# A gather turned round, padded code between experts, and a ring of 21 weight tiles in a mixture-of-experts kernel

## The chip, the cores and the metric

The kernel runs on one core of one Trainium2 chip. The metric is device time in microseconds (us): 1147.12 us is the median of 3 runs of the kernel before (1146.0 to 1147.28). One execution was taken with the hardware profiler.

## The reference

One layer of a streaming encoder on 256 tokens of 1024 values, all in float32. A first half mixes tokens (a convolution and two kinds of attention behind one projection). The second half, on which nearly all of the time goes, is a mixture of 32 experts of which each token takes four:

```python
h2 = rms_norm(x, norm2_g) * (1 + scale2) + shift2
logits = (xt @ router_w + router_b).astype(jnp.float32)
top_vals, top_idx = lax.top_k(logits, TOP_K)          # TOP_K = 4 of 32
top_w = jax.nn.softmax(top_vals, axis=-1)
...
def expert_step(acc, params):
    w1, b1, w2, b2, gate_e = params
    u = xt @ w1 + b1                                  # w1: 1024 x 2048
    glu = jnp.minimum(u[:, ::2], SWIGLU_LIMIT)
    lin = jnp.clip(u[:, 1::2], -SWIGLU_LIMIT, SWIGLU_LIMIT)
    a = glu * jax.nn.sigmoid(SWIGLU_ALPHA * glu) * (lin + 1)
    out = a @ w2 + b2                                 # w2: 1024 x 1024
    return acc + gate_e[:, None] * out.astype(jnp.float32), None
...
return x + gate2 * moe_ffn(h2, ...)
```

## The kernel before

The first half runs from the start to about 183 us. It loads 24 tiles of `w_ada`, 12 of `w_in` and 4 of `w_out`, each 128 x 2048 float32 (1 MB), computes the modulation vectors on VectorE, and the mixers.

The second half is a loop over 32 experts. An expert has 12 weight tiles of 1 MB: eight of `w1` (`we{e}_0` to `we{e}_7`) and four of `w2` (`we{e}_8` to `we{e}_11`), 384 tiles in all. All these tiles, and the big tiles of the first half, live in one pool, the ring. It has 20 tiles of four kinds: `l` (loads of the first half), `h`, `x` and `c` (its intermediate results). `KINDS` (line 33) says how many of each there are, and the string `RING` (line 34) in which order the weight tiles go through them, so weight tile n takes the place of tile n - 20. `prefetch` (line 849) issues the loads on the SyncE queue (SP), in order: 20 before the loop, then 4 at the start of an expert and 8 near its end. Each load waits until the tile that it overwrites has been read for the last time, and until the load eight before it has landed.

A token sits in a slot of its expert. The main path of an expert works on the first 64 slots. In it, `first` (line 876) makes `u` from four `w1` tiles at a time, on two halves (`u{e}_0`, `u{e}_1`); `turned` (898) transposes the activations `a` into `aT`; `second` (906) makes `o` from the four `w2` tiles; VectorE multiplies `o` by the gate (line 1088). Every second expert, `scatter` (937) adds the results of two experts to the residual (`y`).

Before its main path an expert has a conditional block, `if_more` (1020): when more than 64 tokens chose the expert, `more` (957) does slots 65 to 96 in narrow products (32 columns of weights each), with all twelve tiles of the expert; nested inside stand further blocks for over 96, over 160 and over 224 tokens. The code of these blocks stands in the instruction stream between one expert's main path and the next, and is jumped over where it isn't needed. A branch hint (`hint`, line 803) at the start of an expert's main path tells TensorE's sequencer of the jump at its end.

The change's gather is in `Prepare`. For two experts at a time, a one-hot matrix `oh` (tokens x 2 x 64 slots) picks the tokens' normalised rows `xn2`. `gather` (line 734) computes the picked rows with the model's dimension on the partitions: for each of 8 blocks of 128 values and each of 2 token tiles, a block of `xn2` is the stationary operand and `oh` the moving one, 16 products of 128 x 128 into `self.ps`. `modulated2` (740) then applies scale and shift, and the result `xg` feeds `u`. `prepare` (797) is called inside odd experts for the next two, between `first` and `second`; for experts 0 and 1 the calls stand in the first half.

A scheduler sets the final order on each engine: it lets products run ahead or behind where their inputs are later, so the program's order is close to the written one, and not the same.

## Time and profile before

| What | Value |
|---|---|
| median of 3 runs | 1147.12 us (1146.0 to 1147.28) |
| the profiled execution's own time | 1146.89 us |
| its span, first to last instruction | 1144.9 us |
| TensorE (PE) busy | 1069.5 us, 93% of the span |
| VectorE (DVE) / ScalarE (ACT) busy | 389.2 us / 178.6 us |
| moved by DMA | 449.54 MB, mean 393 GB/s |
| granted TensorE clock, mean | 0.985 |

The span is cut into 40 slices of 28.6 us; a digit is a busy share in tenths. Matmuls overlap in the records, so the start of the next row is a better end for a row than its own length. "x16" counts instructions: a float32 product is two matmul instructions, a transpose one, and each has a weight load (PEld) of its own. The idle time in square brackets stands ahead of the row, with what ended it. "PEq" is TensorE's sequencer, and its line 1021 is the branch of `if_more`.

### The profile page before, as it was taken

To read this page: it belongs to the slowest core of one execution; us is meant where nothing else is said; L and a number is where in the kernel's file an instruction comes from. 1 tells how busy PE (TensorE), PEld (TensorE's weight loads), DVE (VectorE), ACT (ScalarE), POOL (GpSimd) and SP (SyncE) were. 2 spreads that over 40 slices of the span, in tenths; PEclk is the share of its full clock that TensorE was granted. 3 is DMA by queue.
4 is the path that set the end of the run, shared out by engine and by line. 5 is a ranking of instruction groups with operands and counts; after the bars stand their busy time and mean duration, and the time that the engine had idled before them with its cause. 6 is when DMAs were issued, how large, how long until landed. Compare 5 with 4: busy or idle time off the path is not lost. (4 is left out here: it accounts for less than half of the span.)

```text
span 1144.9 us, 14101 instructions
## 1 busy us (share of the span) xinstructions
PE 1069.5 (93%) x5432; PEld 467.1 (41%) x5432; DVE 389.2 (34%) x879; ACT 178.6 (16%) x412; POOL 14.5 (1%) x52
## 2 busy tenths in 40 slices
PE   2999999999989999999999989999999999898987
PEld 2887844343333333433333433434343434242322
DVE  7799933222232223222222222232232322231222
ACT  3458622010101010101010100101010101010100
POOL 1000000000000000000000000000000000000000
PEclk7899999999999999999999989999999999999999
DMA  9888899999987999999999999999999999999992
GB/s 383 360 297 311 331 409 370 416 418 417 418 353 309 417 418 417 418 418 417 417 418 416 419 399 404 419 418 418 417 417 419 417 418 417 411 416 410 416 413 110
DMA packets 62913, 449.54 MB, mean 393 GB/s; under 512 B 6960, under 2 KB 7472, under 8 KB 8624
## 3 DMA queue, kind: packets, MB, share of 16 engines
q1 hardware_dynamic: 62336, 447.11, 95.6%
q8 instruction: 79, 1.29, 0.5%
q10 hardware_dynamic: 432, 0.59, 0.1%
q14 instruction: 66, 0.54, 0.1%
HBM read 446.63 MB, written 1.05 MB: 391 GB/s over the span
## 5 line engine op out<-in xcount | busy, mean ns | idle before, releaser
L83 PE MATMUL u<-we,xg 128*64 128x512 f32 (+1 forms) x2304 | 494.2, 577 | 12.7 <-DMA we<-in_w 11.3
L83 PEld LDWEIGHTS u<-we,xg 128*64 128x64 f32 (+1 forms) x2304 | 154.0, 134 | 299.9 <-issue 260.4
L83 PE MATMUL o<-we,aT 128*64 128x512 f32 x1024 | 236.5, 598 | 3.7 <-DMA we<-in_w 3.3
L891 DVE TENSOR_SCALAR sw<-u 128x256 f32<-128x256 f32 (+1 forms) x68 | 28.3, 417 | 441.6 <-PE u L83 429.5
L892 ACT ACTIVATE sw<-sw 128x256 f32<-128x256 f32 (+1 forms) x68 | 27.9, 411 | 666.8 <-DVE sw L891 666.8
L83 PEld LDWEIGHTS o<-we,aT 128*64 128x64 f32 x1024 | 69.6, 136 | 133.2 <-issue 121.8
L1088 DVE TENSOR_TENSOR o<-o,g 64x512 f32<-64x512 f32 x64 | 44.1, 689 | 162.2 <-PE o L83 161.7
L83 PE MATMUL y<-o,sc 128*128 128x512 f32 (+1 forms) x160 | 67.1, 592 | 2.1 <-DVE o L1010 1.3
L83 PEld LDWEIGHTS xg<-oh,xn 128*128 128x128 f32 x512 | 58.6, 192 | 12.6 <-issue 12.4
L83 PE MATMUL xg<-oh,xn 128*128 128x128 f32 x512 | 62.1, 279 | 0.1
L236 DVE SCALAR_TENSOR_TENSOR a<-a,silurow 128x1024 f32<-128x1024 f32 x48 | 57.2, 1216 | 0.0
L745 DVE TENSOR_SCALAR xg<-xg,mods 128x128 f32<-128x128 f32 x64 | 26.0, 410 | 62.7 <-ACT xg L748 61.5
L83 PE MATMUL u<-b,pick 128*128 128x512 f32 x64 | 31.0, 484 | 17.3 <-PEq L1021 16.7
L83 PEld LDWEIGHTS y<-o,sc 128*128 128x128 f32 (+1 forms) x160 | 26.5, 197 | 41.8 <-issue 33.4
L944 DVE TENSOR_TENSOR xr<-xr,y 128x1024 f32<-128x1024 f32 x30 | 36.6, 1221 | 11.8 <-PE y L83 10.4
L904 ACT COPY aT<-aT 128x256 f32<-128x256 f32 x64 | 23.8, 372 | 106.1 <-PE aT L86 106.0
L748 ACT ACTIVATE xg<-xg,mods 128x128 f32<-128x128 f32 x64 | 28.9, 457 | 56.4 <-PE xg L83 45.9
L83 PEld LDWEIGHTS u<-b,pick 128*128 128x128 f32 x64 | 12.1, 189 | 57.1 <-issue 55.9
L86 PEld LDWEIGHTS aT<-ident,a 128*128 128x128 f32 x128 | 14.2, 141 | 50.7 <-issue 33.9
L895 DVE TENSOR_TENSOR a<-a,sw 128x256 f32<-128x256 f32 x64 | 27.4, 428 | 6.8 <-ACT sw L892 0.3
L86 PE MATMUL aT<-ident,a 128*128 128x128 f32 x128 | 27.2, 294 | 2.0
L83 PE MATMUL op<-o,yT 128*128 128x512 f32 x64 | 29.0, 600 | 0.0
(299 smaller groups left out, 750.3 us busy)
## 6 DMA issues: line engine op xcount, KB each, us to landing
we<-in_w SPq DMA_DIRECT2D x383, 1024.0 KB, 19.9
a<-in_ada SPq DMA_DIRECT2D x24, 1024.0 KB, 7.0
w<-in_win SPq DMA_DIRECT2D x12, 1024.0 KB, 11.0
o<-in_wout SPq DMA_DIRECT2D x4, 1024.0 KB, 5.8
xr<-in_x SPq DMA_DIRECT2D x1, 1024.0 KB, 5.3
we<-in_w SPq DMA_DIRECT2D x2, 512.0 KB, 18.1
b1in<-in_be SPq DMA_DIRECT2D x1, 512.0 KB, 5.3
out<-xr SPq DMA_DIRECT2D x2, 256.0 KB, 2.0
```

What stands on the lines that cost most here:

```text
L83: last[:] = [nc.tensor.matmul(out, lhsT, rhs, start=start, stop=stop, skip_group_check=True).ins]
L86: last[:] = [nc.tensor.transpose(out, in_, ident).ins]
L236: nc.vector.scalar_tensor_tensor(w[:, i], w[:, i], 1.0, silu_row, op0=ALU.mult, op1=ALU.mult, accum_out=mods[:, m, k:k + 1])
L745: nc.vector.tensor_scalar(o, x, s2[:, k:k + 1], t2[:, k:k + 1], op0=ALU.mult, op1=ALU.add)
L748: nc.scalar.activation(o, x, AF.Identity, scale=s2[:, k:k + 1], bias=t2[:, k:k + 1])
L891: nc.vector.tensor_scalar(gl, u[:, 0:n], 7.0, None, op0=ALU.min)
L892: nc.scalar.activation(sg, gl, AF.Sigmoid, scale=1.702)
L895: nc.vector.tensor_mul(ln, ln, sg)
L904: nc.scalar.copy(aT.rearrange("p j s -> p (j s)"), ps[:, 0:n])
L944: nc.vector.tensor_add(xr[:, t, :], xr[:, t, :], y.rearrange("p h m -> p (h m)"))
L1088: nc.vector.tensor_mul(o[64 * (e % 2):64 * (e % 2) + 64, 512 * h:512 * h + 512], ps[r, :], g2[r, :])
```

## The change

Three parts. The ring gets an eighth tile of kind `l`, 21 in all, with a new order. The gather of experts 2 to 31 (`beside`) makes `oh` the stationary operand and 512 columns of `xn2` the moving one: 4 products into a second pair of PSUM banks (`xs`), two copies of 128 x 512 to SBUF on ScalarE, and 8 transposes into the place where `gather` wrote. The innermost conditional block of each expert gets a given number of further transposes of the identity (`FILL`), which run only for an expert with over 224 tokens; they lengthen the code that is jumped over, so that main paths begin at multiples of 256 TensorE instructions.

```diff
-KINDS = {"l": 7, "h": 8, "x": 2, "c": 3}
-RING = "lhhllccchlhhhxhhlllx"
+KINDS = {"l": 8, "h": 8, "x": 2, "c": 3}
+RING = "llhhllccchhhhxxhhllll"
...
+FILL = (99, 1, 93, 100, 107, 116, 107, 115, 107, 116, 107, 115, 107, 116, 107, 115, 107, 116, 107, 115, 107, 116, 107, 115, 107, 116, 107, 115, 107, 116, 107, 0)
...
+        def beside(self):
+
+            at = pa(f"xs{self.e}")
+            for t in range(NT):
+                onehot(self.oh[:, t], 0, CAP, [self.e, self.e + 1], pos[:, t])
+            for h in range(2):
+                for t in range(NT):
+                    mm(at[:, h, :], self.oh[:, t].rearrange("p e c -> p (e c)"), xn2[:, t, h * 512:h * 512 + 512], t == 0, t == NT - 1)
+            for h in range(2):
+                xs = t2k(f"xs{self.e}_{h}")
+                nc.scalar.copy(xs, at[:, h, :])
+                for k in range(4):
+                    turn(self.ps[h][:, k * P:(k + 1) * P], xs[:, k * P:(k + 1) * P])
...
     def prepare(e):
         p = Prepare(e)
-        for t in range(NT):
-            p.half(t)
+        p.beside()
         p.rest()
...
             if blocks[1:]:
                 if_more(n_e, e, a, aT, blocks[1:])
+            elif FILL[e]:
+                fill = pb(f"fill{e}")
+                for _ in range(FILL[e]):
+                    turn(fill[:, 0:P], ident)
```

On TensorE, in the main path of expert 1, the gather for experts 2 and 3 stood before as one run between the second `u` and the first `o` (a row "x16" counts products here):

```order
L83 MATMUL u1_1_3021<-we1_7_1671,xg0_1602 64x512 x4
L83 MATMUL xg2_3061<-oh2_3060,xn2_246 128x128 x16
L86 MATMUL og2_3096<-ident_80,og2_3089 128x128 x2
L1051 TENSOR_LOAD cnt_1525
L83 MATMUL o1_3103<-we1_8_2372,aT1_0_2407 64x512 x4
L86 MATMUL aT1_1_3108<-ident_80,a1_1_3040 128x128 x2
L83 MATMUL o1_3103<-we1_9_2374,aT1_0_2407 64x512 x4
```

Now, on the same engine at the same place:

```order
L86 MATMUL u1_1_3125<-we1_7_1671,xg0_1602 64x512 x4
L86 MATMUL xs2_3166<-xn2_246,oh2_3164 128x512 x4
L89 MATMUL og2_3201<-ident_80,og2_3194 128x128 x2
L1071 TENSOR_LOAD cnt_1525
L86 MATMUL o1_3208<-we1_8_1673,aT1_0_2509 64x512
L89 MATMUL xg2_3165<-ident_80,xs2_0_3173 128x128 x4
L89 MATMUL xg2_3165<-ident_80,xs2_1_3179 128x128 x4
L86 MATMUL o1_3208<-we1_8_1673,aT1_0_2509 64x512 x3
L89 MATMUL aT1_1_3213<-ident_80,a1_1_3144 128x128 x2
L86 MATMUL o1_3208<-we1_9_2474,aT1_0_2509 64x512 x4
```

The gather is split: its products stay where they were, and the transposes stand behind one product of `o`, with the other three of that tile after them. Elsewhere TensorE's order is the same, but for the fill inside the blocks that are jumped over.

On SP's queue, the end of the first prefetch and the first branch before (`cnt` is the tile with the tokens' counts, which SP reads for its own branches):

```order
L858 DMA we1_6_1669<-in_w1 128x2048
L858 DMA we1_7_1671<-in_w1 128x2048
L1051 TENSOR_LOAD cnt_1525
L1021 COMPARE_AND_BRANCH x4
L1021 UNCONDITIONAL_BRANCH x5
```

And now:

```order
L874 DMA we1_6_1669<-in_w1 128x2048
L874 DMA we1_7_1671<-in_w1 128x2048
L874 DMA we1_8_1673<-in_w2 128x2048
L1071 TENSOR_LOAD cnt_1525
L1037 COMPARE_AND_BRANCH x4
L1037 UNCONDITIONAL_BRANCH x5
```

The 21st load, tile 8 of expert 1, moved ahead of SP's first branch; from the branch of expert 2 on, as many loads stand before each of SP's branches as before.

## Rows read from the trace of the kernel before

**Rows 1.** The page's picture of the span in 40 slices: TensorE, the DMA engines, and what they moved.

```profile
PE   2999999999989999999999989999999999898987
...
DMA  9888899999987999999999999999999999999992
GB/s 383 360 297 311 331 409 370 416 418 417 418 353 309 417 418 417 418 418 417 417 418 416 419 399 404 419 418 418 417 417 419 417 418 417 411 416 410 416 413 110
```

**Rows 2.** Busy time in six stretches of the loop over experts. Columns: stretch, its length, then busy us and instructions of PE, PEld, DVE, ACT and POOL, the granted clock, the DMA engines' busy share, GB/s.

```profile
183.00:323.00 140.00, 138.35 (x621) 52.27 (x620) 34.24 (x80) 14.38 (x34) 2.54 (x6) 1.00 1.00 411
323.00:349.00 26.00, 21.78 (x259) 10.09 (x259) 10.93 (x29) 1.42 (x5) 0.00 (x0) 0.93 0.63 259
370.00:650.00 280.00, 273.03 (x1250) 102.79 (x1246) 72.62 (x161) 25.89 (x65) 2.66 (x10) 1.00 1.01 418
650.00:705.00 55.00, 47.86 (x354) 18.64 (x352) 15.39 (x33) 3.00 (x9) 0.00 (x0) 0.91 0.99 400
...
975.00:1121.00 146.00, 130.23 (x572) 45.87 (x570) 32.49 (x70) 11.63 (x30) 0.53 (x2) 1.00 1.01 411
1121.00:1134.00 13.00, 11.05 (x49) 3.25 (x47) 1.60 (x4) 0.79 (x2) 0.00 (x0) 1.00 0.07 30
```

**Rows 3.** TensorE in order of time: the first row of the extra block of expert 5 and, behind its last, the start of the expert's main path. Columns: start, length, operation, instructions, idle time ahead.

```profile
323.00 1.07 PE L83 MATMUL xg<-xn,ox 128*32 128x256 f32 x16
...
344.68 0.47 PE L83 MATMUL u<-b,pick 128*128 128x512 f32 x1 [0.67 <-PEq L1021]
345.08 8.75 PE L83 MATMUL u<-we,xg 128*64 128x512 f32 x32
```

**Rows 4.** What SP's queue waited for between 300 and 360 us: line, whom it waited for, us in total, times, the longest.

```profile
SPq L858 <- PE u L83: 45.2, 13, 24.2
```

**Rows 5.** The DMA view of 335 to 352 us, in 40 slices of 0.425 us.

```profile
GB/s 386 386 501 366 405 405 328 308 251 212 154 96 96 77 19 0 0 0 0 0 0 0 39 0 19 0 0 0 0 0 0 0 0 0 154 77 270 386 424 443
```

**Rows 6.** The chain of waits at the end of the span: start, length, what.

```profile
1112.57 19.88 DMA we<-in_w
1132.44 0.14 issue
1132.58 3.67 PE o L83 x16
...
1136.27 0.69 DVE o L1088
...
1137.01 3.91 PE y L83 x8
```

**Rows 7.** TensorE in order of time through a gather (expert 1, for experts 2 and 3).

```profile
226.61 3.84 PE L83 MATMUL xg<-oh,xn 128*128 128x128 f32 x32
230.28 0.38 PE L86 MATMUL og<-ident,og 128*128 128x128 f32 x2
230.60 1.94 PE L83 MATMUL o<-we,aT 128*64 128x512 f32 x8
232.47 0.44 PE L86 MATMUL aT<-ident,a 128*128 128x128 f32 x2
```

**Rows 8.** TensorE in order of time at two places with operations like the new ones: eight transposes in the first half, and four products with 512 moving columns in a scatter.

```profile
162.33 1.04 PE L86 MATMUL h2ps<-ident,xr 128*128 128x128 f32 x8
163.28 3.70 PE L83 MATMUL op<-o,yT 128*128 128x512 f32 x8
...
304.31 3.70 PE L83 MATMUL y<-o,sc 128*128 128x512 f32 x8
307.85 0.38 PE L86 MATMUL aT<-ident,a 128*128 128x128 f32 x2
```

**Rows 9.** Groups of ScalarE operations on 128 x 512, from PSUM and from SBUF: busy us, mean ns of one, idle time ahead.

```profile
L178 ACT ACTIVATE qksq<-qkss,epsc 128x512 f32<-128x512 f32 x6 | 4.1, 686 | 2.8 <-PE qkss L83 2.8
L324 ACT ACTIVATE qksq<-pr 128x512 f32<-128x512 f32 x6 | 3.6, 599 | 11.4 <-PE pr L83 11.4
```

**Rows 10.** TensorE's waits at the branch over the whole span, and the rows in order of time behind the branches of experts 1 to 4 and 10.

```profile
PE u L83 <- PEq L1021: 16.7, 30, 2.0
...
206.78 3.64 PE L83 MATMUL o<-we,aT 128*64 128x512 f32 x14 [0.28 <-PEq L1021]
238.60 0.47 PE L83 MATMUL u<-b,pick 128*128 128x512 f32 x1 [0.40 <-PEq L1021]
268.64 0.49 PE L83 MATMUL u<-b,pick 128*128 128x512 f32 x1 [0.30 <-PEq L1021]
296.90 0.47 PE L83 MATMUL u<-b,pick 128*128 128x512 f32 x1 [0.41 <-PEq L1021]
485.82 0.47 PE L83 MATMUL u<-b,pick 128*128 128x512 f32 x1 [1.99 <-PEq L1021]
```

**Rows 11.** Every wait for a DMA by TensorE, VectorE or ScalarE in the first half (0 to 183 us), by the waits of that stretch.

```profile
ACT silu L216 <- DMA p<-in_p: 3.1, 1, 3.1
ACT win0h L109 <- DMA w<-in_win: 3.0, 1, 3.0
ACT win6h L109 <- DMA w<-in_win: 3.0, 1, 3.0
DVE gains L293 <- DMA p<-in_p: 2.6, 1, 2.6
ACT xn L263 <- DMA xr<-in_x: 0.7, 1, 0.7
```

**Rows 12.** TensorE's waits for projection weights in the first half, the largest near 91 us.

```profile
90.62 0.39 PE L83 MATMUL pr<-hTh,win5h 128*128 128x256 f32 x1 [0.43 <-ACT win5h L109]
91.88 0.39 PE L83 MATMUL pr<-hTh,win5l 128*128 128x256 f32 x1 [0.76 <-DVE win5l L110]
```

**Rows 13.** TensorE in order of time in the extra block of expert 16, at its `w2` tiles.

```profile
665.32 1.07 PE L83 MATMUL o<-we,aTm 128*32 128x256 f32 x16 [0.52 <-DMA we<-in_w]
...
667.91 1.07 PE L83 MATMUL o<-we,aTm 128*32 128x256 f32 x16 [1.26 <-DMA we<-in_w]
670.31 1.07 PE L83 MATMUL o<-we,aTm 128*32 128x256 f32 x16 [1.33 <-DMA we<-in_w]
```

**Rows 14.** The page's row of the queue that fetches code in packets of 16 KB (packets, MB, share of 16 engines' span).

```profile
q8 instruction: 79, 1.29, 0.5%
```

## The prediction

> **What bounds the kernel now.** I read the slices first: from slice 13 on the DMA engines stand at full share nearly everywhere, at 416 to 419 GB/s, and TensorE at nine tenths [rows 1]. Two engines that both look full can't both be the limit, so the next views ask which one waits. The stretches [rows 2] show the DMA at 418 GB/s over 280 us, and real holes in three places: 259 GB/s in 323 to 349, a dent to 400 in 650 to 705, and 30 after 1121. At 418 GB/s a tile of 1.0486 MB takes 2.51 us, an expert's twelve 30.1 us.

> The large hole is one mechanism. Expert 5 has over 64 tokens; its extra block holds TensorE from 323.00 to about 344 [rows 3]. That block reads the expert's tiles, but gives none back, because the main path reads them again. So SP waits once for 24.2 us on a product of `u` [rows 4], and the DMA runs dry near 341 and moves next to nothing until 349.6 [rows 5]. The first place that comes free is that of tile 0 of expert 5, after eight instructions of the row at 345.08. From there on 384 - 80 = 304 loads are left (20 ring places and 60 tiles of five experts), 304 x 2.51 = 763 us, and they would land at 349.6 + 763 = 1113.

> The chain of waits [rows 6] shows the last load landing at 1132.4, with 12.5 us of work behind it that no part of the change touches. Between 1113 and 1132 lies the other finding: after 1121 only 30 GB/s move [rows 2], about a sixteenth of 418 (26). One of 16 DMA engines is late, and a load has landed only when all sixteen are done. That one sets the pace of the loads since 349.6; the dents at 650 and behind 975 are the other fifteen waiting for it or for places. I infer this from the two rows; nothing shows the late engine by name.

> So the end follows from when TensorE first gives a tile back after its extra block in expert 5, and from how many loads are left then. TensorE's own slack later is large: it waits for loads at the end.

> **The change part by part.**

> *21 places.* While TensorE stands in the block, the ring takes one tile more, so 303 loads are left at the restart: -2.5 us. The orders show that nothing on SP's queue stops it: as many loads stand ahead of SP's later branches as before. If the 21st load were held up it would be 0.

> *Ring order and the eighth load tile in the first half.* Loads start earlier there, but nobody waits for them: TensorE has no such wait, ScalarE and VectorE 12.4 us together, all but early ones for the first tiles [rows 11]. I take 0. The bound is the two idle times for weights at 91 us, 0.43 + 0.76 [rows 12]: -1.2 us; upward +1, were the new order to hold a load back.

> *The gather.* Before, 226.61 to 230.28: 3.67 us [rows 7]. After, four products with 512 columns: 3.54 us, as between 304.31 and 307.85; eight transposes: 0.95 us, as between 162.33 and 163.28 [rows 8]. That is 4.49, +0.8. The copies start when all four products are done, since the built program signals once for the four; they take 0.60 to 0.69 us each [rows 9], one behind the other, say until 3.54 + 0.2 + 1.2 = 4.9. TensorE does `og` (0.32) and one product of `o` (a quarter of 1.87, 0.47) meanwhile and the first four transposes, and is at 4.8: a wait of 0.1 to 0.3. I take +1.0 per gather; bounds +0.8 (copies hidden) and +1.6 (both waited for). Two gathers, in experts 1 and 3, lie before the restart: +2.0 us (+1.6 to +3.2). The gathers from expert 5 on delay TensorE alone, which has slack, with one exception: in expert 5 the queue has just restarted and is short, and SP's next load waits behind the gather. It could leave the DMA idle for up to the same 1.0 us; the late engine has more work queued than the others, so I take +0.2. ScalarE's and VectorE's part behind the gather starts later by about 1.3 us, under the 7 us of `o` that follow.

> *The code.* At the branch TensorE idles 16.7 us in 30 places; four of the five before the restart read 0.28 to 0.41, and the fifth, behind the extra block, 0.67 [rows 3, 10]. They are nearly the same wherever the target lay, so I read them as the price of the jump, not of the place of the code: 0. Bounds: all five go, -2.06; or each becomes like the one of 1.99 us in expert 10, 5 x 1.6 = +8. The 1.99 us of expert 10 lie behind the restart, where TensorE has slack, and are worth nothing. The fill itself never runs.

> [...]

> **Sum:** -2.5 + 0 + 2.0 + 0.2 + 0 = -0.3 us. Against the profiled execution's own 1146.89 (0.2 under the median): 1146.6 us.

> **The rivals.** A measurement of this kernel tells about 0.2%, 2.3 us, from no change; faster begins at 1144.8, slower at 1149.4.

> *The dent counts, or the jumps get cheaper.* If the dent of 650 to 705 is a real stop for the late engine too, it is worth 55 x (418 - 400) / 418 = 2.4 us, and the extra place fills it. Against: the block of expert 16 itself waits 3.1 us for loads [rows 13], so TensorE is barely behind there, and it will come later by its gathers. Or the five idle times go. Either gives 1146.6 - 2.4 = 1144.2 or 1146.6 - 2.1 = 1144.5; with the first half's 1.2 us too, 1143.0.

> [...]

> *The 21st place does not count.* The load after tile 79 waits for something else in expert 5's block, and the gathers remain: 1146.6 + 2.5 = 1149.1, or 1150.3 with gathers at 1.6.

> **How the numbers follow.** No change as summed, 1145.0 to 1149.2: 0.45. The first rival: 0.32. Jumps that wait, from two on: 0.15. No 21st place: 0.08, most of it near or over the slower bound. So faster 0.33, same 0.45, slower 0.22. The range goes from 1143.2 (first rival with its extras) to 1150.4 (two long waits, or the dear gather without the place).

> **What would show it.** Right: SP's longest wait in expert 5's block again a single one, near 24 us or shorter by the load that came before it; restart of the DMA about 2 us later than 349.6, from the gathers; the last load landing at about 1132. A gather of 4.5 to 5.3 us between the second `u` and the end of the transposes, less `og` and the product between. Branch idle times unchanged at 0.3 to 0.4. Wrong: a restart not later than 349.6 with one load fewer left (faster by the whole tile); a stretch 650 to 705 at 418 GB/s together with an earlier end; branch idle times of over 1 us before 350; TensorE without waits for loads behind 1000 us, which would mean that it, not the DMA, had become the bound.

## The result and the profile after

The changed kernel takes 1160.09 us against 1147.2, medians of four runs each; the ratio is 1.011, with a 95% interval of 1.0092 to 1.0128. It is slower by some 13 us, and the predicted 1146.6 us and its range are missed. The profiled execution took 1159.73 us (span 1157.8); the reading below is of that one.

The page's picture of the span, for [rows 1]:

```profile
PE   2999999899999999999999978999999999999997
...
DMA  9988899999995999999999997999999999999993
GB/s 382 392 295 320 329 392 391 376 385 387 417 404 222 382 414 419 417 418 418 418 417 417 418 413 284 419 418 417 418 417 418 419 417 418 416 417 419 419 417 153
```

The hole of expert 5 (222 GB/s) is still there. The dent of expert 16, which was 399 and 404 in [rows 1], has become a hole too (284), and TensorE has a seven and an eight there in place of an eight and a nine. TensorE's waits over the whole span (whom for, us in total, times, the longest) say why:

```profile
PE u L86 <- PEq L1037: 18.4, 30, 5.5
...
PE o L86 <- PEq L1037: 4.0, 1, 4.0
...
PE o L86 <- DMA we<-in_w: 1.0, 2, 0.7
```

PEq, L1037 is TensorE's own sequencer at the branch. In [rows 10] the longest such wait was 2.0 us; now there is one of 5.5 and one of 4.0. The waits for loads, of which the kernel before has 17.7 us, 3.1 of them in expert 16 and the rest behind 900 us, are down to two, 1.0 us together. Before:

```profile
PE u L83 <- DMA we<-in_w: 11.3, 14, 1.5
PE o L83 <- DMA we<-in_w: 6.4, 10, 1.3
```

In order of time, the three places that matter: the jump from expert 0 to 1, the gather in expert 1, and the way out of the extra blocks of experts 5 and 16.

```profile
210.76 6.05 PE L86 MATMUL o<-we,aT 128*64 128x512 f32 x14 [4.00 <-PEq L1037]
216.73 0.50 PE L86 MATMUL u<-b,pick 128*128 128x512 f32 x1
...
233.00 3.70 PE L86 MATMUL xs<-xn,oh 128*128 128x512 f32 x8
236.53 0.38 PE L89 MATMUL og<-ident,og 128*128 128x128 f32 x2
236.84 1.07 PE L86 MATMUL o<-we,aT 128*64 128x512 f32 x2
237.85 1.09 PE L89 MATMUL xg<-ident,xs 128*128 128x128 f32 x8
238.87 1.93 PE L86 MATMUL o<-we,aT 128*64 128x512 f32 x6
240.73 0.44 PE L89 MATMUL aT<-ident,a 128*128 128x128 f32 x2
...
354.81 0.47 PE L86 MATMUL u<-b,pick 128*128 128x512 f32 x1 [0.66 <-PEq L1037]
...
697.70 0.77 PE L86 MATMUL u<-b,pick 128*128 128x512 f32 x1 [5.49 <-PEq L1037]
698.40 9.72 PE L86 MATMUL u<-we,xg 128*64 128x512 f32 x32
```

The first row answers to that of 206.78 in [rows 10]: the wait has grown from 0.28 to 4.00 us, and the 14 instructions behind it take 6.05 us where they took 3.64. The windows tell that this is the clock (columns as in [rows 2]):

```profile
207.00:217.00 10.00, 6.24 (x15) 1.83 (x15) 1.35 (x7) 0.00 (x0) 0.00 (x0) 0.66 0.79 294
...
334.00:360.00 26.00, 21.79 (x250) 9.95 (x247) 10.20 (x28) 1.42 (x5) 0.00 (x0) 0.93 0.51 202
360.00:690.00 330.00, 320.71 (x1493) 112.75 (x1489) 84.83 (x192) 37.26 (x91) 3.19 (x12) 1.00 1.01 413
690.00:708.00 18.00, 12.49 (x43) 4.12 (x41) 2.23 (x4) 0.00 (x0) 0.00 (x0) 0.62 0.62 242
708.00:1125.00 417.00, 410.01 (x1694) 140.97 (x1694) 108.10 (x234) 45.23 (x109) 3.19 (x12) 1.00 1.01 416
```

Over the pause of 4.0 us and the 6 us behind it the granted clock averages 0.66: in windows of 1 us it reads 0.50 from 210 to 215 us, 0.69 in the next and 1.00 from 216 us on. So the one jump costs 6.1 us: 3.7 of wait and 2.4 of clock. In 690 to 708 the DMA moves 242 GB/s and loses 18 x (418 - 242) / 418 = 7.6 us; TensorE is busy for 410 of the 417 us behind it.

The chain of waits needs care here. Its end reads as before:

```profile
1104.59 19.89 DMA we<-in_w
...
1124.54 20.85 DMA we<-in_w
1145.39 0.14 issue
1145.52 3.67 PE o L86 x16
```

By the chain alone the last load still sets the end. But a load is issued only when TensorE gives a place back, and TensorE had no idle time for loads until then: the two arrive together.

### The profile page after: what moved, and what is told of

Read it like the earlier page. It is cut to its first block, busy times and chain, and to the rows that moved or that the text cites. A ratio compares the mean times of both kernels' runs of the same rounds, so it can differ in the third digit from the quotient of the medians.

```text
span 1157.8 us, 13666 instructions
## 1 busy us (share of the span) xinstructions
PE 1093.7 (94%) x5192; PEld 451.8 (39%) x5192; DVE 389.1 (34%) x879; ACT 194.5 (17%) x442; POOL 14.5 (1%) x52
## 5 line engine op out<-in xcount | busy, mean ns | idle before, releaser
L86 PE MATMUL o<-we,aT 128*64 128x512 f32 x1024 | 253.8, 603 | 5.1 <-PEq L1037 4.0
L86 PEld LDWEIGHTS o<-we,aT 128*64 128x64 f32 x1024 | 73.0, 138 | 137.7 <-issue 133.3
L86 PE MATMUL xs<-xn,oh 128*128 128x512 f32 x120 | 55.5, 605 | 0.0
L86 PEld LDWEIGHTS xs<-xn,oh 128*128 128x128 f32 x120 | 21.6, 190 | 33.7 <-issue 33.7
```

Source lines behind the costliest of these rows:

```text
L86: last[:] = [nc.tensor.matmul(out, lhsT, rhs, start=start, stop=stop, skip_group_check=True).ins]
```

## The experiments

Three theories were at hand. The one that the trace suggests: the gather is dearer than forecast, and two jumps wait for code; what lies ahead of the restart in expert 5 delays the DMA at once, and what lies behind makes TensorE late enough in expert 16 that the ring is full when its extra block begins, so that the DMA stops a second time. The rivals: the new order of the ring is the loss, or one of the three parts alone is.

**The parts one by one.** `e1_ring21` has on the kernel before the new ring alone:

```diff
-KINDS = {"l": 7, "h": 8, "x": 2, "c": 3}
-RING = "lhhllccchlhhhxhhlllx"
+KINDS = {"l": 8, "h": 8, "x": 2, "c": 3}
+RING = "llhhllccchhhhxxhhllll"
```

> The kernel before with the new ring of 21 alone (old gather, no fill). Theory (the ring gains one load at the restart, the loss comes from the gather and from jumps that wait for code): restart of the DMA still near 349.6 us, one load fewer left, 2.5 us off: 1144.2 to 1145.0. First rival (the 21st place does not count): 1147 within 0.5. Second rival (the new order of tiles in the ring is itself the loss, loads wait for the wrong places): 1152 or more, with TensorE waiting for loads between 400 and 900 us.

Measured 1144.62 us against 1146.68 (ratio 0.998, 0.997 to 0.999): 2.1 us off. The ring does what it should, and this is the fastest kernel of the study.

`e2_gather` has the new gather alone (`p.beside()` in place of the two `p.half(t)`):

> The kernel before with the new gather alone (ring of 20, no fill). Theory: the gather costs 1.88 us in each odd expert, two of them before the restart, so the DMA restarts 3.8 us later and, while it stays the bound, the end is 3.8 us later: 1151; up to 1154 if TensorE, which has lost about 13 us behind expert 16, uses up all its waits for loads at the end (some 14 us before). The jump from expert 0 to expert 1 waits less than 2 us. Rival (the gather alone is the whole loss): 1158 or more. Rival (the gather is hidden by TensorE's slack): 1147 to 1148.

Measured 1157.02 (1.0086, 1.0055 to 1.0116), above the theory's 1151 to 1154 and near the first rival. Expert 5's main path begins at 348.12 us, 3.4 later than in [rows 3], near the 3.8 expected. What I had not expected is in expert 16, at the same jump as in the changed kernel, and without any fill. The kernel before first, then this one:

```profile
677.16 0.77 PE L83 MATMUL u<-b,pick 128*128 128x512 f32 x1 [0.66 <-PEq L1021]
...
682.92 2.19 PE L83 MATMUL y<-o,sc 32*128 32x256 f32 x12 [0.20 <-DVE o L1023]
691.12 0.77 PE L83 MATMUL u<-b,pick 128*128 128x512 f32 x1 [6.01 <-PEq L1034]
```

So the fill does not make this wait. In its 6 us the DMA view shows one packet on the queue that fetches code:

```profile
q8 instruction: 1, 0.02, 1.1%
```

`e3_nofill` is the changed kernel with `FILL = (0,) * 32`, `e4_ring20` the changed kernel with the old two lines of `KINDS` and `RING`.

> The changed kernel with all fills at zero, so that the main paths begin wherever the code ends: new ring and new gather. Theory (a good third to a half of the loss is the place of the code): the waits of 4.0 us at the jump from expert 0 to 1 with its lowered clock, and of 5.5 us behind expert 16's extra block, go; 1147.2 - 2.5 + 3.8 = 1148.5, between 1148 and 1151.5. Rival (the fill changes nothing, gather and ring are the loss): 1158 to 1160, with the same long waits at the jumps.

> The changed kernel with the old ring of 20 and its old order: new gather and fill. Theory: TensorE is the bound of the changed kernel from the jump behind expert 16's extra block on, so one tile more or less in the ring changes little: 1160 to 1162.6 (2.5 us, if the restart still counts in part). Rival (the new order of the ring is the loss): 1152 or less. The long waits of 4.0 and 5.5 us at the two jumps stay in their places, if they come from the place of the code alone, which the ring does not change on TensorE.

Measured 1158.14 (1.0092, 1.0074 to 1.011) and 1161.8 (1.0129, 1.0105 to 1.0154). In `e3_nofill` the jump of expert 0 waits 0.28 us as before and expert 5's main path begins at 348.61, 6.2 us ahead of the changed kernel's 354.81. Yet that is worth only 2 us at the end, and the theory's 1148.5 is missed; the rival's 1158 came, though not with the same waits. The wait behind expert 16 stays (5.95 us), and four of the other jumps wait 1.1 to 2.2 us, which with the fill all read 0.40 but for that of expert 6 (1.56). Over the whole span the jumps wait 23.4 us without the fill and 22.4 with it. The old ring makes nothing better, so its new order is not the loss. The fill alone, on the kernel before, was not run.

**Where a dear gather counts.** In `e5_early` only experts 1 and 3 gather in the new way, in `e6_late` only experts 17 to 29:

```diff
-        p.beside()
+        if e <= 4:
+            p.beside()
+        else:
+            for t in range(NT):
+                p.half(t)
```

(in `e6_late` the condition is `e >= 18`).

> The kernel before with the new gather only in experts 1 and 3, the two that lie ahead of the restart of the DMA. Theory: the restart comes 3.4 to 3.8 us later, every load behind it too, and nothing else changes: 1146.7 + 3.6 = 1150.3 (1149.9 to 1150.7); the wait behind expert 16's extra block stays at 0.7 us. Rival (only what lies behind expert 16 counts, since TensorE becomes the bound there): 1146.5 to 1147.3.

> The kernel before with the new gather only in experts 17 to 29 (seven gathers, all behind expert 16). Theory: 7 x 1.88 = 13.2 us of TensorE against some 14 to 17 us in which it waited for loads behind expert 16, so nearly all hidden: 1146.7 to 1148.5, the waits for loads at the end almost gone. Rival (the late gathers alone make TensorE the bound and carry the loss): 1153 or more.

Measured 1151.29 (1.0037, 1.0024 to 1.0051), 3.6 us more, and 1147.73 (0.9997, 0.9988 to 1.0007), no change. TensorE's waits of the late ones, whole span:

```profile
PE o L83 <- DMA we<-in_w: 4.6, 5, 1.3
...
PE u L83 <- DMA we<-in_w: 0.2, 1, 0.2
```

Seven gathers have used up slack, down to 4.8 us of waits, and cost nothing. The two early ones cost their full 2 x 1.88. One expectation fell: in `e5_early` the jump behind expert 16 waits 5.61 us, not 0.7, and this costs nothing seen at the end, since TensorE still waits 15.9 us for loads in this run. The early two are 3.6 of the gather's 10 us, the late seven by themselves 0. No run has the six of experts 5 to 15 alone; the next two runs tell what part of the rest is theirs.

**The wait behind expert 16.** `e7_flat16` takes away the jump, `e9_hint` gives its target ahead; both are the gather alone otherwise.

```diff
-        if_more(n_e, e, t1k(f"am{e}", "partp"), t1k(f"aTm{e}"))
+        if_more(n_e, e, t1k(f"am{e}", "partp"), t1k(f"aTm{e}"), MORE[:1] if e == 16 else MORE)
```

```diff
+        label = {0: f"few{e}", 1: f"end{e}" if e == 16 else None}.get(MORE.index(blocks[0]))
+        with tc.If(n_e > blocks[0][0], label=label) if label else tc.If(n_e > blocks[0][0]):
+            if e == 16 and blocks is MORE:
+                tc.mark_branch_hint_location("end16", "LikelyTaken", [mybir.EngineType.PE])
```

> The run of the gather alone (1157.0 us), with the code for more than 96 tokens left out in expert 16, which the given inputs do not reach: its extra block now runs straight into the main path, with no jump over 2000 instructions. Theory (the 6.0 us behind the extra block are a wait for code, and TensorE is the bound behind it): that wait falls under 1 us and the end comes 4.5 to 5.3 us earlier, 1151.7 to 1152.5, not under 1150.3, where the loads bind. First rival (the wait is for the code but the loads set the end anyway): wait gone, 1156 to 1157. Second rival (the 6 us are not the jump, but something that the block leaves behind): the wait stays near 6 us and so does the time.

> The run of the gather alone (1157.0 us), with a hint at the head of expert 16's extra block that names the target of its own exit, as the kernel already gives one for each expert's entrance. Nothing else is changed, the jump over the code for more than 96 tokens stays. Theory (the 6.0 us are a fetch that begins only when the jump is taken): a fetch appears while the block runs, the wait falls under 1 us, and the time is that of the run with the block flat, 1152 to 1153.5. Rival (the code is fetched in time and the jump chain itself costs the 6 us, or the hint is too early and its block is given up again): wait and time stay, 1156 to 1158.

Measured 1153.13 (1.0045, 1.0028 to 1.0061) and 1153.23 (1.0051, 1.0035 to 1.0068) against 1157.02, whose four runs lie 7 us apart; two later runs with the same wait (`e13_less2`, `e14_less8`) read 1156.37 and 1156.46. Behind the extra block of the one there is no idle time, and of the other 0.73 us:

```profile
686.58 0.51 PE L83 MATMUL u<-b,pick 128*128 128x512 f32 x1
...
687.22 0.47 PE L83 MATMUL u<-b,pick 128*128 128x512 f32 x1 [0.73 <-PEq L1035]
```

So the 6 us go with the jump, and a hint takes them to 0.73; with the packet that lies in them I read them as a wait for code. 3.8 us of them come through to the end, somewhat less than forecast. Whether an extra fetch runs while the block does, as I expected, stays open: in 664 to 690 us, from the start of the extra block on, q8 has two packets in `e2_gather` and three in `e9_hint`, over the whole span 76 and 75. Which code a packet holds, the trace does not tell.

The second hole goes with the wait. The pages of `e2_gather` and, with all fifteen gathers in it as well, `e7_flat16`:

```profile
GB/s 382 357 297 322 332 394 382 418 406 410 418 331 296 382 418 418 418 418 418 417 418 416 421 376 318 417 418 419 417 418 418 418 417 420 418 418 416 419 416 153
...
GB/s 383 353 299 311 334 401 373 417 414 401 418 357 273 385 419 417 417 418 417 418 417 419 418 400 400 419 418 417 418 417 418 417 419 417 418 414 411 415 412 112
```

Where `e2_gather` has 376 and 318, `e7_flat16` has 400 and 400, as the kernel before has 399 and 404 [rows 1]. In `e9_hint` they are 390 and 376, in `e5_early`, with the wait but less lateness, 385 and 361. So the lateness of TensorE by the gathers does not make the hole by itself, and neither does the pause; both together do. Without the pause the gather alone costs 5.4 us (1153.13 against the 1147.70 of that comparison) or, with the hint, 6.0 (against 1147.24). The early two make 3.6 of that, so the thirteen gathers from expert 5 on cost some 2 us together, about what these runs can tell from nothing.

**The split of a pair.** In the rows above, the eight transposes stand between the first product of `o` and the other three. `e8_unsplit` moves them behind all four (and the modulation with them), where the transposes of `aT` already stood:

```diff
-        second(ps, e, 0, aT[0], CAP, lambda: turned(a, CAP, aT[1], f"{e}_1"))
+        second(ps, e, 0, aT[0], CAP, lambda: (turned(a, CAP, aT[1], f"{e}_1"), p and (p.turns(), p.rest())))
```

> The run of the gather alone (1157.0 us), with its eight transposes moved behind the first four products of o, to the place where the transposes of aT already stand, so that the second column half of a product stays beside its first. Theory (about 1.0 of the 1.88 us per gather is the split of the pair, 0.9 the gather itself): an odd expert takes 0.8 to 1.0 us more than before instead of 1.88, the restart is 1.8 us later than before, TensorE saves about 1 us in each of 15 gathers and the loads bind again at the end: 1148.5 to 1151. Rival (the 1.88 us are the gather's own work and its wait for the copies): no saving, 1156 or more.

```profile
226.30 3.70 PE L83 MATMUL xs<-xn,oh 128*128 128x512 f32 x8
229.93 1.94 PE L83 MATMUL o<-we,aT 128*64 128x512 f32 x8
231.80 0.44 PE L86 MATMUL aT<-ident,a 128*128 128x128 f32 x2
232.07 1.04 PE L86 MATMUL xg<-ident,xs 128*128 128x128 f32 x8
232.94 0.38 PE L86 MATMUL og<-ident,og 128*128 128x128 f32 x2
233.26 5.37 PE L83 MATMUL o<-we,aT 128*64 128x512 f32 x24
...
680.91 0.77 PE L83 MATMUL u<-b,pick 128*128 128x512 f32 x1 [0.67 <-PEq L1039]
```

Measured 1151.05 (1.0029, 1.0019 to 1.004): 6 us off. The eight records of `o` take 1.87 us from start to start in one piece; split, 1.01 + 1.86 = 2.87. Two records are one product with 64 stationary columns, and the eight are two pairs: a pair takes 1.87 / 2 = 0.94 us, not much more than one product with 128 stationary columns (3.54 / 4 = 0.89 [rows 8]). So I read the two of a pair as running side by side. The one product ahead of the transposes takes 1.01 us by itself, and its partner behind them, in the 1.86 us of a pair and a product, another 0.93: each alone takes as long as a pair. From the first row of the second `u` to the next jump expert 1 takes 21.54 us (217.48 to 239.02), against 22.69 in `e2_gather` and 20.79 in the kernel before. So the gather itself costs 0.75 us, and the split the rest of the 1.9. The wait behind expert 16 is gone as well, which I had not foreseen, so not all of the 6 us is the split.

**The jump of expert 0.** `e10_start0` is the changed kernel with `FILL[0]` at 35 instead of 99 and `FILL[1]` at 65 instead of 1, so that expert 0's main path alone moves, by 128 instructions. `e11_after_hint` is the changed kernel with the hint of `e9_hint`. `e12_mended` has both, and the moved transposes.

> The changed kernel with the main path of expert 0 alone moved by 128 instructions (fill of expert 0 64 products of identity shorter, that of expert 1 64 longer, so that every other path stays where it is). Theory (the 4.0 us at the jump from expert 0 to 1 come from where expert 0's path lies, and its lowered clock from the pause): the wait falls under 1 us, expert 1 begins 6 us earlier (near 210.5), expert 5's main path near 348.7; with TensorE the bound to the end, 1160.1 - 5 to 6.2 = 1154 to 1155. Rival (the wait hangs on the place of its target, expert 1's path, which does not move here): wait and time stay at 4.0 and 1160. Rival (the loads set the end): wait gone, 1158 or more.

> The changed kernel with the hint for expert 16's exit alone. Theory: the wait of 5.5 us falls under 1 us, the 4.0 us at expert 0 stay; TensorE is the bound, 1160.1 - 4.8 = 1155.3 (1154.5 to 1156.5). Rival (the hint does nothing): 1159.5 to 1161.

> The changed kernel with all three at once: expert 0's path moved by 128 instructions, the hint for expert 16's exit, and the gather's transposes behind the first four products of o. Theory (these three and the gather's own 0.8 us are the whole of the loss): the loads bind again, 1147.2 - 2.3 for the ring + 2 x 0.8 for the two gathers ahead of the restart = 1146.5 (1145.5 to 1147.5), TensorE waits for loads at the end. Rival (something of the change is still unaccounted for): 1149 or more.

Measured 1153.12 (1.0051), 1156.58 (1.0082) and 1148.38 (1.0006, 0.9996 to 1.0016). In `e10_start0`:

```profile
207.05 3.64 PE L86 MATMUL o<-we,aT 128*64 128x512 f32 x14 [0.28 <-PEq L1037]
210.62 0.50 PE L86 MATMUL u<-b,pick 128*128 128x512 f32 x1
```

The wait and the lowered clock are gone, 7.0 us at the end, a little more than forecast. The target of the jump has not moved; the path that leads to it has, and the skipped code between them is longer. In 186 to 206 us the DMA view of the changed kernel has no packet on q8, that of `e10_start0` has this one:

```profile
q8 instruction: 1, 0.02, 0.3%
```

In the changed kernel the packet comes when TensorE stands already: one lies in its wait, 206.7 to 210.8 us, and begins 1.2 us after TensorE's last work. `e11_after_hint` saves 3.5 us, a little under the forecast. With all three mended the change is no slower than before by what can be measured, and TensorE waits for loads again:

```profile
PE u L86 <- DMA we<-in_w: 9.4, 12, 1.5
PE o L86 <- DMA we<-in_w: 2.8, 6, 0.7
```

It is 1.1 us over the kernel before, where 0.7 less was forecast. Nearly as much is missing in `e8_unsplit`, 3.4 us over the kernel before with two gathers of 0.8 ahead of the restart. Part of it is seen: in both, the granted clock is down for longer near the first product of expert 5's main path than in the kernel before. In the two halves of 340 to 360 us it reads 0.72 and 0.94 in `e8_unsplit`, 0.85 and 0.81 in `e12_mended`, where the kernel before has 0.83 and 1.00. The 32 records of `u` behind that product take 9.15 and 9.61 us against 8.75 in [rows 3], which delays the first place that is given back by about 0.4 us. In the profiled execution of `e12_mended` the loop also begins later, at 184.58 us against 182.79, without a known cause: in the runs with one of the three edits each it begins between 182.5 and 183.1. The rest stays open.

**What decides whether a jump waits.** `e2_gather` waits 6.01 us behind expert 16 and `e8_unsplit` 0.67, though by the built programs their code lies within one instruction of the same place. `e13_less2` and `e14_less8` are `e2_gather` with 127 and 124 never executed products of identity at the end of expert 15's conditional code (2 and 8 instructions earlier, counted modulo 256 as by the change's fill), `e15_plus2` is `e8_unsplit` with one such product (2 later). That the hardware keeps to this unit, no run shows.

> The run of the gather alone, with 127 products of identity (254 instructions, never executed) at the end of the code for more than 224 tokens of expert 15, so that all code from expert 15's main path on lies 2 instructions earlier in its block of 256. Theory A (the wait behind expert 16's extra block hangs on where its code lies, to the instruction: the run with the transposes moved, in which it lay 1 instruction earlier, waited 0.67 us, the gather alone 6.01): the wait falls to 0.7 us, the time to 1152.5 to 1154. Theory B (it hangs on TensorE's order or on whether the loads hold it up, not on 2 instructions): the wait stays at 5.5 to 6 and the time at 1156 to 1158.

> The same with 124 products of identity, 8 instructions earlier in the block; the kernel before, in which that code lay 7 instructions earlier than in the gather alone, waited 0.66 us. Theory A: 0.7 us of wait, 1152.5 to 1154. Theory B: 5.5 to 6 us, 1156 to 1158.

> The run with the transposes moved (1151.05 us, wait 0.67), with one product of identity at the same place, so that the code from expert 15 on lies 2 instructions later in its block. Theory A: the wait behind expert 16's extra block rises to 5.5 to 6 us; the time rises little, since TensorE waits there for loads that set the pace, 1151 to 1153. Theory B: the wait stays at 0.7, the time at 1151.

Measured waits 6.02, 6.12 and 0.67 us; times 1156.37, 1156.46 and 1150.81. Theory A falls: here 2 and 8 instructions do not matter. Among the runs that have the jump and no hint there, it is cheap where TensorE waits for a load in the extra block (the kernel before, `e1_ring21`, `e6_late`, `e8_unsplit`, `e15_plus2`) and dear where it does not (the changed kernel, `e2_gather`, `e3_nofill`, `e4_ring20`, `e10_start0`, `e13_less2`, `e14_less8`). That is agreement, not a cause shown, and one run breaks it: `e5_early` has in experts 15 and 16 the order of the kernel before, and waits for loads in the extra block as that does, and yet:

```profile
685.69 0.76 PE L83 MATMUL u<-b,pick 128*128 128x512 f32 x1 [5.61 <-PEq L1038]
```

By its two gathers (32 instructions of products, transposes and weight loads each, where the old gather has 64) its code lies, modulo 256, some 64 instructions away from where it lies in the cheap and the dear runs without fill. A shift of that size was not tried at this jump, so it may play a part. The cause of this one wait stays open, its price and its cure do not.

## Why the prediction was wrong

- **The ring: right.** 2.5 us were forecast, 2.1 measured alone. The dent of 650 to 705 us [rows 2] fills from 400 to 412 GB/s in that run, and the time does not fall further, so the first rival's 2.4 us for it are not there. That one late DMA engine sets the end, and that a load has landed only with the last of sixteen, the prediction infers from [rows 2] and [rows 6]; no run tests it.
- **First half at 0: right.** The loop begins at 183.06 us against 182.79; in the other profiled runs it lies between 182.4 and 184.6.
- **The gather, +1.0 each: mis-sized.** It is 1.88, outside its bounds of 0.8 to 1.6. The products (3.53 us) and the transposes (1.02) came as read from [rows 8], and the wait for the copies does not appear at all. What the sum missed is in a row that it used itself, the eight records of `o` in 1.94 us [rows 7]: a quarter of that, 0.47, is right for a product only while its partner stands next to it in the order, and I had put the transposes behind a single product. The order shows this place, and the rows beside it gave the price: products of 512 moving columns that have no partner take 3.54 / 4 = 0.89 us [rows 8].
- **"The gathers from expert 5 on delay TensorE alone, which has slack": wrong at the gather's true price.** The kernel before has 17.7 us of waits for loads (11.3 + 6.4). Thirteen gathers at 1.0 would have stayed under that; at 1.88 they are 24.4 and use it up, down to 1.3 us in `e7_flat16`. TensorE waits for loads in expert 16's extra block [rows 13], and I took this as a sign that it is barely behind; six gathers more than use up these 3.1 us. By itself that costs little, some 2 us in `e7_flat16` and `e9_hint`, and the late seven alone cost nothing. But it takes away what would hide a pause: the wait behind expert 16 costs nothing seen in `e5_early`, where 15.9 us of waits for loads are left, and 3.8 us and a second hole in `e2_gather`, where 0.2 are left.
- **The code, 0: the step that failed most.** I read the 0.28 to 0.41 us of [rows 10] as the price of a jump wherever it leads. It is the price of most jumps. Two others, with a packet on q8 inside the wait, cost 4.0 us and 2.4 of clock ahead of the restart, and 5.5 behind expert 16. In the trace of the kernel before, waits of 1.06 and 2.03 us stand at 513.05 and 708.18 us beside the 1.99 of [rows 10], and the mean of all but the longest, (16.7 - 2.0) / 29 = 0.5, hid them. The forecast gave "Jumps that wait, from two on" a chance of 0.15 and took their price from the longest wait of that trace, 1.6 us over the common one. No run with the fill shows two jumps at that price ahead of the restart: in the changed kernel one jump there waited 4.00 us and the other four 0.30 to 0.66, and the 5.49 stand behind expert 16.
- **What would show it.** TensorE without waits for loads behind 1000 us was named as the sign that it had become the bound. It came but for the last 1.0 us. So did "branch idle times of over 1 us before 350", with the 4.0 us at 210.76. The restart of the DMA, forecast 2 us behind 349.6, came near 359.4, some 10 us later: 3.8 for the two gathers and 6.1 for the jump.

Of the 13 us, then, mending the jump of expert 0 gives back 7.0 and the hint 3.5, each alone; mending the gather's order as well leads to 1148.4.

## What to carry to other kernels

Slack is a matter of place and of sum: a cost on an engine that is not the bound is paid in full ahead of a long hold of the ring, and behind it it is free only while all such costs together stay under what the engine waits. Before code is moved, look in the trace for the largest wait at a jump and ask whether the moved jumps may become like it, and count what a pause costs beside its length, since the clock fell behind the one at expert 0 (2.4 us beside 3.7). Keep the two narrow products of a pair next to each other when something is put between products (splitting one pair cost 1.0 us here), and give a hint for the way out of a conditional block too, not only for its entrance (6.01 us became 0.73 here).
